# The small products of head pairs, chained in the order in which they are issued

## The chip, the cores and the metric

The kernel runs on one core of a Trainium2 chip. A time is the number of device microseconds (us) of one execution; of several executions the median is given. In the profile PE is TensorE, DVE is VectorE, ACT is ScalarE, POOL is GpSimd and SP is SyncE, whose queue issues most of the transfers.

## The reference: one hybrid decoder layer

The input x has 256 tokens of 2048 features, all float32. The layer is

```
x = x + 0.5 * swiglu(rms_norm(x))                       # feed-forward 1, inner width 5632
p = rms_norm(x) @ w_in                                  # all projections of the mixer
y_attn = sliding_window_attention(q, k, v, sinks)       # 16 heads of 64, 4 key heads, window 128
y_rwkv = rwkv7_time_mix(p_rwkv)                         # 16 heads of 64, a recurrence over tokens
x = x + (gate_a * (y_attn @ w_a) + gate_r * (y_rwkv @ w_r)) @ w_out
x = x + cross_attention(rms_norm(x), rms_norm(mem))     # 4 heads of 128 into 256 memory rows
x = x + 0.5 * swiglu(rms_norm(x))                       # feed-forward 2
out = rms_norm(x)
```

The recurrence of one head keeps a 64 x 64 state S and does, token by token,

```
sa = S a_t ;  S = S * w_t + sa b_t^T + v_t k_t^T ;  y_t = S r_t
```

with the decay w and the rate a taken from two low-rank products (`tanh(xw) @ w2` and `xa @ a2`, both of rank 64).

## The kernel before

**The stream.** Nearly all of the arithmetic is products of 256 tokens with large weight matrices. Weights are loaded in pieces of 2 or 4 x 128 rows by 512 columns, each split by ScalarE and VectorE into a rounded part and a remainder (lines 311 and 312), and each product of a piece is three matmuls of 128 rows and 512 columns (lines 399, 400 and 401, in `times`). These three lines are called the stream below. The two feed-forwards use a scheme with seven instead of eight block products; they are not touched.

**What runs beside it.** All smaller work of the mixer (attention, the recurrence, transposes, norms) is written as generators that `bg`, an `Interleave`, advances by one step after each half piece of the stream. So the order in the source is a mixture: a few small matmuls, then six of the stream, then small ones again. The build then has a scheduler that puts the instructions of each engine into a final order by its own estimate of when their operands and buffers are ready; it may move a small matmul past matmuls of the stream. `tc.issue_after(ins)` gives it one more rule: what is traced in the block comes after `ins` in the order of that engine. It adds no wait on a semaphore, and it does not ask that the two be neighbours.

**Head pairs.** Heads are 64 wide, and a feature tile has 128 partitions, so two heads lie in one tile: head e = 0 in partitions 0 to 63 and head e = 1 in 64 to 127. A product that contracts over one head's 64 features uses only 64 rows of the array: rows 0 to 63 (called the low half, L) for e = 0 and rows 64 to 127 (the high half, H) for e = 1. Each head of a pair has its own PSUM bank. At four places such products come in pairs:

- `attend`, line 856: attention scores, per key head and query block 2 x 2 products of 128 or 256 columns (32 in all);
- `decay_and_rate`, line 994: the low-rank products, 4 x 4 products of 256 columns (16);
- `removal_keys`, line 1087: the matrix of the token-by-token system that is later inverted, 4 x 8 products of 128 columns (32);
- `pair`, line 1226: three products for each head, head pair and half of the tokens, 16 groups of 6 products of 128 columns (96).

Operands here are plain float32, and each such product is carried out as two matmul instructions, each with its own weight load: the profile counts 192 matmuls for the 96 products of line 1226.

**What reads them.** After each group VectorE reads the two banks, e = 0 first: line 862 (scores, which the softmax follows), line 1093 (multiplication by the mask), line 1231 (multiplication by three masks, into `mk`); for the low-rank products it is ScalarE, line 1001. The first reader on TensorE of `mk` is line 1240. The banks of a group come from rings: `mm()` has three buffers, `tr()` has two, and both are shared with other small work, so the first product into a bank can have to wait for the last reader of the bank's former content.

**Other small matmuls** beside these groups: lines 596 and 895 are transposes; 903 is the attention output (64 columns of the array each); 1168, 1240 to 1289 are the rest of the recurrence; they use all 128 rows.

The loop of the recurrence, before:

```
for m, (x1, x2) in enumerate(((kh, ah), (kh, rh), (bh, rh))):
    for e, r in enumerate(rows):
        pe.matmul(b[e][:, m * P : (m + 1) * P], x1[r, j, cs_], x2[r, j, cs_], ...)
```

## Time and profile before

| | |
|---|---|
| median of 3 runs | 2266.49 us (2264.76 to 2267.68) |
| the profiled execution | 2266.59 us, of which the span of its instructions 2264.9 us |
| granted TensorE clock in it | 0.999 |
| PE busy | 2248.1 us, 99% of the span |
| DVE, ACT, POOL busy | 1742.6, 1212.8, 129.4 us |
| DMA | 434.63 MB, mean 192 GB/s |

The mixer's scores are computed at about 768 to 817 us from the span's start, the low-rank products at 835 to 849, line 1087 at 895 to 936, and line 1226 at 1090 to 1261.

How it is read: a row of the timeline gives the start, the duration, the engine, the line, the operation, the tiles, the rows and columns of the array, and how many instructions were merged into the row; in square brackets stands idle time of the engine before it, with what ended it. The ends of matmuls are modelled, and they overlap the next ones, so it is the distance from start to start that tells what a matmul costs. A row of the view by stretches gives the stretch (from : to), its length, the busy time of the engine and in brackets how many of its instructions touch the stretch, then the clock and the DMA share.

### The profile page before, as it was taken

The numbers are of one execution on the slowest core, as the hardware profiler recorded it, in microseconds if no ns is written. First come the engines' busy times: TensorE is split into PE (matmuls) and PEld (weight loads), VectorE is DVE, ScalarE is ACT, GpSimd is POOL, SyncE is SP. The second block draws the span as 40 slices with busy tenths as digits, with TensorE's granted clock in tenths as the row PEclk, the third lists the DMA queues.
The fourth block names the chain that finished last, engine by engine and source line by source line (L and its number), as shares of the span: only waits on it lengthen the run. The fifth ranks groups of instructions, "written<-read, shape, count | busy, mean of one in ns | idle before, by whom it ended". The sixth has DMA issues, their size and how long they took to land.

```text
span 2264.9 us, 28302 instructions
## 1 busy us (share of the span) xinstructions
PE 2248.1 (99%) x10588; PEld 1843.7 (81%) x10588; DVE 1742.6 (77%) x2120; ACT 1212.8 (54%) x1611; POOL 129.4 (6%) x184
## 2 busy tenths in 40 slices
PE   9999999999999999999999999999999999999998
PEld 7888888888888778888888888888888888888886
DVE  7988988888986567795444566647898888898887
ACT  6555555545555576444344446556555455555554
POOL 1000000000000002201220030001000000000002
PEclk9999999999999999999999999999999999999999
DMA  7666665566666545766433577647665665666664
GB/s 244 213 223 196 204 205 190 184 215 196 200 205 195 142 142 161 236 209 195 116 108 88 170 258 235 194 159 261 195 204 186 205 204 186 194 197 204 202 201 155
DMA packets 219435, 434.63 MB, mean 192 GB/s; under 512 B 13745, under 2 KB 15873, under 8 KB 219297
## 3 DMA queue, kind: packets, MB, share of 16 engines
q1 hardware_dynamic: 210768, 406.37, 56.2%
q0 software_dynamic: 7952, 25.65, 3.6%
q8 instruction: 83, 1.36, 0.2%
q10 hardware_dynamic: 576, 0.79, 0.1%
q14 instruction: 56, 0.45, 0.1%
HBM read 419.65 MB, written 13.11 MB: 191 GB/s over the span
## 4 chain that ended last, share of the span: by engine, by line
PE 92%; DVE 3%; DMA 2%; issue 1%; ACT 1%; SPq 0%; POOLq 0%; POOL 0%; ACTq 0%; DVEq 0%
PE acc L399 19%; PE acc L400 19%; PE acc L401 19%; PE mm L400 8%; PE mm L401 8%; PE mm L399 8%; PE tr L596 2%; PE tr L400 2%; PE tr L401 2%; PE tr L399 1%; DVE lo L312 1%; PE mm L1257 1%; PE tr L1226 1%; DMA raw<-in_ffn_w_up_dram 1%; ACT hi L311 1%
## 5 line engine op out<-in xcount | busy, mean ns | idle before, releaser
L311 ACT CAST hi<-raw 128x1024 fp32r<-128x1024 f32 (+1 forms) x770 | 763.6, 1000 | 787.8 <-PE acc L401 394.5
L312 DVE TENSOR_TENSOR lo<-raw,hi 128x1024 fp32r<-128x1024 f32 (+1 forms) x770 | 891.2, 1168 | 370.5 <-ACT hi L311 369.2
L399 PE MATMUL acc<-hi,xhi 128*128 128x512 f32 (+1 forms) x1196 | 477.0, 400 | 1.3 <-ACT hi L311 1.0
L400 PE MATMUL acc<-lo,xhi 128*128 128x512 f32 (+1 forms) x1196 | 465.6, 389 | 0.8 <-DVE lo L312 0.8
L401 PE MATMUL acc<-hi,xlo 128*128 128x512 f32 (+1 forms) x1196 | 464.9, 389 | 0.0
L399 PEld LDWEIGHTS acc<-hi,xhi 128*128 128x128 f32 x1196 | 225.0, 188 | 51.3 <-issue 5.4
L401 PEld LDWEIGHTS acc<-hi,xlo 128*128 128x128 f32 x1196 | 225.0, 188 | 47.0 <-issue 0.6
L400 PEld LDWEIGHTS acc<-lo,xhi 128*128 128x128 f32 x1196 | 225.3, 188 | 46.3 <-issue 2.7
L336 ACT CAST thi<-raw 128x1024 fp32r<-128x1024 f32 x160 | 166.0, 1051 | 72.2 <-DVE raw L331 35.6
L337 DVE TENSOR_TENSOR tlo<-raw,thi 128x1024 fp32r<-128x1024 f32 x160 | 192.8, 1219 | 1.1 <-ACT thi L336 1.1
L400 PE MATMUL acc<-lo,hhi 128*128 128x512 f32 x404 | 157.9, 391 | 0.0
L401 PE MATMUL acc<-hi,hlo 128*128 128x512 f32 x404 | 157.8, 391 | 0.0
L399 PE MATMUL acc<-hi,hhi 128*128 128x512 f32 x404 | 157.2, 392 | 0.0
L399 PE MATMUL mm<-hi,xhi 128*128 128x512 f32 x380 | 149.1, 392 | 0.0
L400 PE MATMUL mm<-lo,xhi 128*128 128x512 f32 x380 | 148.1, 390 | 0.0
L401 PE MATMUL mm<-hi,xlo 128*128 128x512 f32 x380 | 148.1, 390 | 0.0
L331 DVE TENSOR_TENSOR raw<-raw 128x1024 f32<-128x1024 f32 x80 | 97.6, 1220 | 23.6 <-DMA raw<-in_ffn_w_up_dram 22.1
L400 PEld LDWEIGHTS acc<-lo,hhi 128*128 128x128 f32 x404 | 75.8, 188 | 17.5 <-DVE lo L312 2.3
L399 PEld LDWEIGHTS acc<-hi,hhi 128*128 128x128 f32 x404 | 75.9, 188 | 16.0 <-DVE x L554 0.9
L401 PEld LDWEIGHTS acc<-hi,hlo 128*128 128x128 f32 x404 | 75.9, 188 | 15.3
L400 PEld LDWEIGHTS mm<-lo,xhi 128*128 128x128 f32 x380 | 71.4, 188 | 15.3 <-DVE lo L312 0.4
L401 PEld LDWEIGHTS mm<-hi,xlo 128*128 128x128 f32 x380 | 71.3, 188 | 14.7
(374 smaller groups left out, 3409.5 us busy)
## 6 DMA issues: line engine op xcount, KB each, us to landing
raw<-in_ffn_w_gate_dram SPq DMA_DIRECT2D x167, 512.0 KB, 3.8
raw<-in_ffn_w_up_dram SPq DMA_DIRECT2D x160, 512.0 KB, 4.7
raw<-in_ffn_w_down_dram SPq DMA_DIRECT2D x152, 512.0 KB, 4.8
raw<-in_w_in_dram SPq DMA_DIRECT2D x136, 512.0 KB, 3.7
raw<-in_w_out_dram SPq DMA_DIRECT2D x32, 512.0 KB, 4.5
raw<-in_ffn_w_down_dram SPq DMA_DIRECT2D x12, 1024.0 KB, 5.1
raw<-in_ffn_w_up_dram SPq DMA_DIRECT2D x8, 1024.0 KB, 6.3
raw<-in_w_proj_attn_dram SPq DMA_DIRECT2D x16, 512.0 KB, 3.8
```

The source lines that it names most:

```text
L311: newest["act"] = act.copy(hi[:, s], raw[:, s])
L312: newest["dve"] = dve.tensor_tensor(lo[:, s], raw[:, s], f32(hi[:, s]), ALU.subtract)
L331: dve.tensor_tensor(ta[:], raw[:, 1:3], raw[:, 0:2], ALU.subtract)
L336: act.copy(hi[:, s], t[:])
L337: dve.tensor_tensor(lo[:, s], t[:], f32(hi[:, s]), ALU.subtract)
L399: pe.matmul(o, xh, hi, start=first, stop=False, **how)
L400: pe.matmul(o, xh, lo, start=False, stop=False, **how)
L401: pe.matmul(o, xl, hi, start=False, stop=last, **how)
L596: pe.transpose(b[:, o : o + P], tok[:, t, col : col + P], ident[:])
L1226: pe.matmul(b[e][:, m * P : (m + 1) * P], x1[r, j, cs_], x2[r, j, cs_], start=True, stop=True,)
L1257: pe.matmul(vb[:, o : o + P][:, r], lhs(e), rhs[:, r], start=first and e == 0, stop=True, **ek,)
```

## The change

The products of each of the four places are handed to a new function, which gives each product after the first the rule to come after the one before it. And the head with e = 1 now comes first in each pair. The number of products, their operands, their results and the readers stay the same.

```diff
+    def by_turns(products):
+        prev = None
+        for args in products:
+            with tc.issue_after(prev.ins) if prev else nullcontext():
+                prev = pe.matmul(*args, start=True, stop=True)
 
@@ attend
-            for c in range(2):
-                for e in range(2):
-                    r = slice(64 * e, 64 * e + 64)
-                    pe.matmul(
-                        b[e][:, c * w : (c + 1) * w], qt[kv // 2][r, 2 * (kv % 2) + c, tq],
-                        kd[r, kv, :w], start=True, stop=True,
-                    )
+            by_turns(
+                (
+                    b[e][:, c * w : (c + 1) * w],
+                    qt[kv // 2][64 * e : 64 * e + 64, 2 * (kv % 2) + c, tq],
+                    kd[64 * e : 64 * e + 64, kv, :w],
+                )
+                for c in range(2) for e in (1, 0)
+            )
@@ decay_and_rate
-                    for i in range(2):
-                        for e in range(2):
-                            r, c = slice(64 * e, 64 * e + 64), (4 * h + q + i) * P
-                            pe.matmul(
-                                b[e][:, i * T : (i + 1) * T], wa[r, c : c + P], xwa[r, :],
-                                start=True, stop=True,
-                            )
+                    by_turns(
+                        (
+                            b[e][:, i * T : (i + 1) * T],
+                            wa[64 * e : 64 * e + 64, (4 * h + q + i) * P : (4 * h + q + i + 1) * P],
+                            xwa[64 * e : 64 * e + 64, :],
+                        )
+                        for i in range(2) for e in (1, 0)
+                    )
@@ removal_keys
-                for j in range(4):
-                    for e in range(2):
-                        r = slice(64 * e, 64 * e + 64)
-                        pe.matmul(
-                            b[e][:, j * P : (j + 1) * P], at_[h][r, j, cs_], bt[h][r, j, cs_],
-                            start=True, stop=True,
-                        )
+                by_turns(
+                    (
+                        b[e][:, j * P : (j + 1) * P], at_[h][64 * e : 64 * e + 64, j, cs_],
+                        bt[h][64 * e : 64 * e + 64, j, cs_],
+                    )
+                    for j in range(4) for e in (1, 0)
+                )
@@ pair
-                for m, (x1, x2) in enumerate(((kh, ah), (kh, rh), (bh, rh))):
-                    for e, r in enumerate(rows):
-                        pe.matmul(
-                            b[e][:, m * P : (m + 1) * P], x1[r, j, cs_], x2[r, j, cs_],
-                            start=True, stop=True,
-                        )
+                by_turns(
+                    (b[e][:, m * P : (m + 1) * P], x1[r, j, cs_], x2[r, j, cs_])
+                    for m, (x1, x2) in enumerate(((kh, ah), (kh, rh), (bh, rh)))
+                    for e, r in ((1, rows[1]), (0, rows[0]))
+                )
```

## The prediction

> **What bounds the kernel now.** I read the page first (busy time, then the chain that ended last), then the stretch of the recurrence, then TensorE's timeline around one group of each kind.

> ```profile
> PE 2248.1 (99%) x10588; PEld 1843.7 (81%) x10588; DVE 1742.6 (77%) x2120; ACT 1212.8 (54%) x1611; POOL 129.4 (6%) x184
> ...
> PE 92%; DVE 3%; DMA 2%; issue 1%; ACT 1%; SPq 0%; POOLq 0%; POOL 0%; ACTq 0%; DVEq 0%
> ```

> TensorE is busy all the time and carries 92% of the chain. In the view by stretches the recurrence, where 96 of the 176 touched products lie, is tighter still:

> ```profile
> 1085.00:1265.00 180.00, 179.83 (x1175) 149.52 (x1174) 80.53 (x106) 76.58 (x172) 22.90 (x38) 1.00 0.35 99
> ```

> Busy times stand here in the order PE, PEld, DVE, ACT, POOL: TensorE lacks 0.17 of 180 us, VectorE works 80.53. So there the time is the sum of distances from one matmul's start to the next, and a shorter distance moves all that follows.

> **What a group costs.** One group of line 1226 that already alternates, in TensorE's timeline:

> ```profile
> 1089.71 0.39 PE L401 MATMUL acc<-hi,xlo 128*128 128x512 f32 x1
> 1090.03 0.49 PE L1226 MATMUL tr<-at,aa 64*128 64x128 f32 x4
> 1090.36 0.39 PE L1226 MATMUL tr<-rt,aa 64*128 64x128 f32 x4
> 1090.58 0.39 PE L1226 MATMUL tr<-rt,kk 64*128 64x128 f32 x4
> 1090.90 0.50 PE L399 MATMUL acc<-hi,xhi 128*128 128x512 f32 x1
> 1091.23 0.39 PE L400 MATMUL acc<-lo,xhi 128*128 128x512 f32 x1
> 1091.47 0.40 PE L401 MATMUL acc<-hi,xlo 128*128 128x512 f32 x1
> ```

> The stream steps by about 0.23. Into the group it takes 0.32, out of it 0.33 to the second matmul: a visit to 64-row products costs its own stretch (first start to the next product's start) and about 0.20 beside (0.32 + 0.33 less two steps). Now the stretches, one row each, PE's count also taking in neighbours that run into the stretch. Recurrence:

> ```profile
> 1090.03:1090.90 0.87, 0.87 (x13) 1.00 0.87 306
> 1093.37:1094.24 0.87, 0.87 (x8) 1.00 0.89 346
> 1095.36:1096.22 0.86, 0.86 (x7) 1.00 0.00 0
> 1098.66:1100.22 1.56, 1.56 (x14) 1.00 0.24 93
> 1120.98:1122.60 1.62, 1.62 (x14) 1.00 0.05 10
> 1126.29:1127.90 1.61, 1.61 (x13) 1.00 0.00 0
> 1145.27:1146.69 1.42, 1.42 (x15) 1.00 0.00 0
> 1164.81:1165.22 0.41, 0.41 (x3) 1.00 0.33 80
> 1165.64:1166.28 0.64, 0.64 (x6) 1.00 0.73 147
> 1166.94:1167.80 0.86, 0.86 (x7) 1.00 1.04 331
> 1188.25:1189.82 1.57, 1.57 (x14) 1.00 0.57 220
> 1205.58:1206.77 1.19, 1.19 (x14) 1.00 0.49 33
> 1207.66:1208.53 0.87, 0.87 (x13) 1.00 1.00 386
> 1213.37:1214.93 1.56, 1.56 (x13) 1.00 0.00 0
> 1255.57:1255.98 0.41, 0.41 (x3) 1.00 0.00 0
> 1259.79:1260.65 0.86, 0.86 (x7) 1.00 0.72 210
> ```

> Six products in turns (first row) take 0.87; three of one half alone also take 0.86 to 0.87: the partner is free. Three of one half and then three of the other take 1.42 to 1.62, or 1.19 where H could start under the L products; one product alone takes 0.41, two 0.64. The scheduler of before turned the source's L H L H L H into L L L H H H in ten of the 16 groups (in three of these with other matmuls between the parts), since the second head's bank comes free later. What such a group costs hangs on when that is.

> **The change, part by part.** No instruction is added or removed on any engine; POOL's and SP's queues are in the same order, transfers included. As built, a few casts and small operations of ACT and DVE change places with a neighbour. What moves is on TensorE. [...]

> *Recurrence (line 1226).* As built, six of the 16 groups are H L H L H L without a gap; in ten the first H stands alone, one to 14 other matmuls follow, then L H L H L together. In the ten that costs 0.41 + 0.87 and two visits, 1.68 in all (the five last ones by three products of one half, the partner free). Group by group, visits included, before and after:

> - first, fourth, ninth, 14th, 15th: in turns before and after, 1.07, no change;
> - second (0.87 and 0.86 apart): 2.13 to 1.68, -0.45; third: 1.76 to 1.68, -0.08; fifth: 1.82 to 1.68, -0.14; sixth: 1.81 to 1.07, -0.74; seventh: 1.62 to 1.68, +0.06;
> - eighth and 16th (0.41, 0.64 and 0.86 apart, three visits): 2.51 to 1.68, -0.83 each;
> - tenth and 13th: 1.77 and 1.76 to 1.68, -0.17 together;
> - eleventh (1.19): 1.39 to 1.68, +0.29; twelfth (0.87): 1.07 to 1.68, +0.61. These two lose.

> Sum -2.3. The wait for the second bank doesn't go: in 1098.66 to 1100.22 it lay behind three L products; now other matmuls lie there, and L after them comes no earlier than the H of before did.

> *Matrix to invert (line 1087).* Two visits for each half of the heads, and VectorE's first masked multiply in each:

> ```profile
> 895.85:897.83 1.98, 1.98 (x25) 1.00 0.18 69
> 898.76:899.85 1.09, 1.09 (x9) 1.00 0.45 120
> 931.75:933.73 1.98, 1.98 (x25) 1.00 0.19 68
> 934.44:935.53 1.09, 1.09 (x9) 1.00 0.46 118
> ```

> ```profile
> 898.03 0.68 DVE L1093 TENSOR_TENSOR lt<-mm,mask_l 128x512 f32<-128x512 f32 x1
> ```

> Before: eight products in turns and four L (1.98), one stream matmul, then four H, which wait for that multiply (it ends at 898.71, they start at 898.76; the second time they start at 934.44, alike). After, as built: nine in turns, four or five stream matmuls, then seven in turns beginning with L. Nine in turns are five of one half: 0.86 + two more products of 0.22 (0.86 less 0.64) = 1.30. The second visit still waits for the same multiply and still takes 1.09 (four of one half), but three and four more stream matmuls are done by then: 7 x 0.23 = -1.6.

> *Scores (line 856) and low rank (line 994).* Stretches of the second and fourth scores, and of one low-rank group:

> ```profile
> 781.62:782.47 0.85, 0.85 (x9) 1.00 0.00 0
> 783.92:785.51 1.59, 1.59 (x9) 1.00 0.70 186
> 810.78:812.07 1.29, 1.29 (x12) 1.00 0.09 27
> 835.64:836.71 1.07, 1.07 (x10) 1.00 0.76 145
> ```

> All four low-rank groups alternate before and after: 0. So do the first and third scores. In the second, L H H of 256 columns (1.59) becomes L H L like the low-rank row (1.07), less 0.20 for a visit that now stands among stream matmuls: -0.3. In the fourth, two L of 256 columns at the end of a visit (1.29) become one (0.85): -0.4. Two blocks of line 903 are also split by a stream matmul before and whole after; by the 0.20 of a visit that is worth between 0 (the second half waits for its copy instead) and -0.4; I take -0.2, as nothing tells.

> Sum: -2.3 - 1.6 - 0.7 - 0.2 = -4.8 us. Its ends: with nothing for line 903 -4.6, with all of it -5.0; the two losing groups and the visits are sums of like rows and have no wider bounds of their own. The profiled execution took 2266.59 (its span 2264.9 and 1.7 around), 0.1 over the median of the three runs, so 2261.8 against it and 2261.7 against the median, 0.21% less.

> [...] The 64-row visits of the recurrence go from 21 to 26. [...] Counted alone it would make the time 5 x 0.20 = 1.0 us longer; it is in the sum already.

> **What could hide or undo it.** The two mask multiplies of line 1231 both come after the group now, where that of e = 0 could run beside H H H before:

> ```profile
> 1091.01 1.02 DVE L1231 TENSOR_TENSOR mk<-tr,mask 128x384 f32<-128x384 f32 x2
> ```

> ```profile
> 1184.95 1.23 DVE L312 TENSOR_TENSOR lo<-raw,hi 128x1024 fp32r<-128x1024 f32 x1 [3.00 <-ACT hi L311]
> ```

> ```profile
> 1186.70 0.32 PE L1240 MATMUL tr<-vtok,mk 128*128 128x64 f32 x1 [0.17 <-DVE mk L1231]
> ```

> In the first group both end at 1092.03, 1.13 after the group's stretch ended; as built the shortest way from a changed group to line 1240 is five stream matmuls (0.33 + 4 x 0.23 = 1.25). That is covered, by 0.12 at the least.

> **Rivals.**
> - *Slower: the masks are late.* Line 1240 waits wherever VectorE is in one of its long subtractions (line 312) when the group ends. One such case, of the ninth group, is the last two rows above. If it meets all eleven regrouped ones in full (1.13 of mask work behind a subtraction of 1.23, less the 1.25: 1.1 us each), that is +12.1 - 4.8 = +7.3: 2273.8. It decides from 0.44 us per group on. Against it: VectorE is idle for more than half of this stretch. 0.12.
> - *Partly lost: it does not do what it says.* The chain orders the products and does not make them neighbours; ten first products stand alone, and were the L after them to wait for its bank, or the last scores, which come eight stream matmuls later, to hold up the transposes at 825.83, half would go:

> ```profile
> 825.83 0.76 PE L895 MATMUL tr<-ident,s 128*128 128x128 f32 x5 [0.80 <-DVE s L889]
> ```

>   -2.4: 2264.1. For it: that wait exists, and the scores' softmax is a chain of VectorE and ScalarE. Against: the reduction of the other block comes ahead as built. 0.18.
> - *More:* the wait of 0.80 goes too, and the two blocks of line 903 give all of 0.4: -4.8 - 0.8 - 0.2 = -5.8: 2260.7. For it: the work on VectorE between the scores and the transposes moves ahead. 0.25.

> **Numbers.** The forecast, 2261.7 give or take 1.2, has 0.45. A measurement tells about 0.2%, 4.5 us, so "faster" begins at 2262.0: most of the forecast's part (0.28) and all of "more" (0.25) are faster, 0.53. The rest of it (0.17) and "partly lost" are the same, 0.35. Slower: 0.12. The range reaches over the forecast, "more" with 2 us for waits outside, and "partly lost" up to 2267: 2258.5 to 2267.

> **What the profile after would show.** Right: the sum of line 1226's stretches about 2 us shorter, no L L L H H H; at 1087 the second visit seven in turns and the same wait; feed-forwards unchanged. Wrong: idle time before line 1240 put down to `mk`, before the second part of a group put down to a copy or mask, or before line 895 longer than 0.80.

## The result, and the profile after

The changed kernel takes 2260.45 us (median of 10 runs, 2258.33 to 2262.48), the kernel before, run beside it, 2265.47 (10 runs, 2264.18 to 2267.68): 5.0 us less, a ratio of 0.9977 with a 95% interval of 0.9967 to 0.9987. The forecast was 4.8 us less. The profiled execution took 2258.33 us, its span 2256.6.

Lines below the new function are 8 to 10 further down than before: the stream is now lines 407 to 409, and all chained products stand under line 177, inside `by_turns`. The page's busy times and its chain, after:

```profile
PE 2240.6 (99%) x10588; PEld 1836.1 (81%) x10588; DVE 1740.8 (77%) x2120; ACT 1213.3 (54%) x1611; POOL 130.9 (6%) x184
...
PE 95%; DVE 3%; issue 1%; ACT 1%; DMA 1%; SPq 0%; POOLq 0%; POOL 0%; ACTq 0%; DVEq 0%
```

TensorE does the same 10588 matmuls, is busy 7.5 us less, and is still busy 99% of the time: the gain lies in how densely its products start, not in idle time taken away.

**Where it came from.** Both kernels issue the same number of matmul instructions in all of these stages, so the time from the start of one fixed instruction, counted from the start of the kernel and standing a few instructions away from a stage, to the start of the next such one can be compared directly. Worked out so from the records of the trace, profiled execution against profiled execution (us):

| stretch | before | after less before | predicted |
|---|---|---|---|
| first feed-forward and what precedes the scores | 765.81 | -1.05 | 0 |
| scores, line 903, low rank | 127.31 | -1.08 | -0.9 |
| matrix (line 1087 of before) | 49.42 | -1.58 | -1.6 |
| matrix to recurrence | 145.21 | 0.00 | 0 |
| recurrence (line 1226 of before) | 176.48 | -1.97 | -2.3 |
| **mixer, the four together** | 498.42 | **-4.63** | **-4.8** |
| all behind the recurrence | 990.84 | -2.57 | 0 |

The profiled pair is 8.3 us apart, more than the medians; the 3.6 us outside the mixer are taken up in the experiments.

**The groups.** Stretches of TensorE after (from : to, length, busy time of PE and the matmul instructions that touch it, clock, DMA share, GB/s), in this order: two visits of the scores, the second low-rank group, the two visits of the first half of the matrix, then the recurrence's first group, its second, sixth, eighth and twelfth:

```profile
783.54:784.60 1.06, 1.06 (x8) 1.00 0.54 185
808.78:809.63 0.85, 0.85 (x9) 1.00 0.09 27
837.23:838.56 1.33, 1.33 (x9) 1.00 0.81 211
893.72:895.03 1.31, 1.31 (x20) 1.00 0.22 83
896.63:897.71 1.08, 1.08 (x14) 1.00 0.47 146
1086.32:1087.19 0.87, 0.87 (x14) 1.00 0.99 351
1089.66:1090.08 0.42, 0.42 (x4) 1.00 1.00 390
1091.66:1092.52 0.86, 0.86 (x12) 1.00 0.00 0
1122.58:1123.72 1.14, 1.14 (x13) 1.00 0.86 212
1159.98:1160.40 0.42, 0.42 (x3) 1.00 0.25 78
1161.98:1162.84 0.86, 0.86 (x11) 1.00 1.06 407
1202.67:1203.09 0.42, 0.42 (x4) 1.00 0.02 5
1203.52:1204.38 0.86, 0.86 (x11) 1.00 0.00 0
```

The reader should see four things. The ten split groups are one product alone (0.42) and then five in turns (0.86 or 0.87), as forecast. The twelfth group, which was whole before (0.87), is now split and loses, also as forecast. The sixth, whole and in turns, takes 1.14 and not 0.87. And the second low-rank group, in turns as before, takes 1.33 where it took 1.07: its second product starts at 837.50, when ScalarE has read its bank (line 1011); in the run with the scores alone, further down, the same group takes 1.33 too, so this is a price of the scores having moved ahead. In the first half of the matrix the second visit still waits for the same VectorE multiplication; in the second half (931.63) no idle time is left before it:

```profile
896.63 1.16 PE L177 MATMUL mm<-kk,at 64*128 64x128 f32 x14 [0.41 <-DVE lt L1103]
```

TensorE's waits in the mixer, in the view of who waited for whom (total, times, longest), before and then after:

```profile
PE tr L895 <- DVE s L889: 0.8, 1, 0.8
PE mm L1087 <- DVE lt L1093: 0.6, 2, 0.4
PE tr L903 <- ACT pt L898: 0.6, 1, 0.6
PE acc L399 <- DVE ga L1140: 0.2, 1, 0.2
PE tr L1240 <- DVE mk L1231: 0.2, 1, 0.2
```

```profile
PE tr L904 <- DVE s L898: 0.7, 1, 0.7
PE tr L912 <- ACT pt L907: 0.6, 1, 0.6
PE mm L177 <- DVE lt L1103: 0.4, 1, 0.4
PE acc L407 <- DVE ga L1150: 0.2, 1, 0.2
PE tr L1249 <- DVE mk L1240: 0.2, 1, 0.2
```

They are the same five, together 0.3 us shorter. The masks `mk` are not late: 0.2 before, 0.2 after.

### The profile page after: what moved, and what is told of

It reads as the page before. It is cut to its first block, busy times and chain, and to the rows that moved or that the text cites. A ratio compares the mean times of both kernels' runs of the same rounds, so it can differ in the third digit from the quotient of the medians.

```text
span 2256.6 us, 28302 instructions
## 1 busy us (share of the span) xinstructions
PE 2240.6 (99%) x10588; PEld 1836.1 (81%) x10588; DVE 1740.8 (77%) x2120; ACT 1213.3 (54%) x1611; POOL 130.9 (6%) x184
## 4 chain that ended last, share of the span: by engine, by line
PE 95%; DVE 3%; issue 1%; ACT 1%; DMA 1%; SPq 0%; POOLq 0%; POOL 0%; ACTq 0%; DVEq 0%
PE acc L407 19%; PE acc L409 19%; PE acc L408 19%; PE mm L408 8%; PE mm L409 8%; PE mm L407 8%; PE tr L604 2%; PE tr L408 2%; PE tr L409 2%; PE tr L407 2%; PE mm L1266 1%; DVE lo L320 1%; PE tr L177 1%; PE mm L177 1%; ACT hi L319 0%
```

## The experiments

Three questions were open. Do the four places add up, or does part of the gain come from elsewhere in the program? Is it the turns themselves that pay, or what the chain does to the time at which the second head's bank is needed? And what is a group worth whose bank is free? A ratio stands with its interval; a kernel without a ratio is one profiled execution.

### One place at a time

**Recurrence alone**: `by_turns` at line 1226 of before; the three other places written as before.

> The chain at line 1226 (recurrence) alone; the other three places as before. Theory of the distances: the change is worth, place by place, what the starts of TensorE's matmuls say, and nothing else. Then the recurrence, 4858th to 5600th matmul, is 2.0 us shorter than before, as in the changed kernel, and the scores and the matrix to invert are as before to 0.1; time 2.0 below before. Rival, the outside: the 3.7 us by which the profiled execution of the changed kernel was also shorter outside the mixer come from the change; then the feed-forwards get shorter here too, by something like 3.7 x 2.0/4.6 = 1.6, in all -3.6.

**Matrix alone** (line 1087 of before).

> The chain at line 1087 (matrix to invert) alone. Distances: the two places together 1.6 us shorter, all else in the mixer as before to 0.1; time 1.6 below before. Outside: feed-forwards shorter as well, by 1.3, in all -2.9.

**Scores alone** (line 856).

> The chain at line 856 (scores) alone. Distances: the attention stretch up to the low-rank products 1.1 us shorter (of it -1.0 in the second block, +0.4 in the fourth, -0.5 behind it, where the last transposes wait), all else as before; time 1.1 below before. Outside: feed-forwards shorter by 0.9 as well.

**Low rank alone** (line 994), where only the leading head changes: a control.

> The chain at line 994 (low rank) alone: as built the same visits with H first. Distances: nothing in any stretch of the mixer, 0 +- 0.1; the time differs from before by what feed-forwards differ between executions. If the order of the two heads counted (H first cheaper than L first), the four visits of 1.07 would change.

The edit is the same for each. For the recurrence alone, against the changed kernel, at one of the three places that go back:

```diff
@@ attend
-            by_turns(
-                (
-                    b[e][:, c * w : (c + 1) * w],
-                    qt[kv // 2][64 * e : 64 * e + 64, 2 * (kv % 2) + c, tq],
-                    kd[64 * e : 64 * e + 64, kv, :w],
-                )
-                for c in range(2) for e in (1, 0)
-            )
+            for c in range(2):
+                for e in range(2):
+                    r = slice(64 * e, 64 * e + 64)
+                    pe.matmul(
+                        b[e][:, c * w : (c + 1) * w], qt[kv // 2][r, 2 * (kv % 2) + c, tq],
+                        kd[r, kv, :w], start=True, stop=True,
+                    )
```

Measured, less before's profiled execution, by the same stretches (us):

| | after | recurrence | matrix | scores | low rank |
|---|---|---|---|---|---|
| scores, line 903, low rank | -1.08 | -0.04 | -0.07 | -1.02 | +0.05 |
| matrix | -1.58 | +0.01 | -1.57 | +0.02 | +0.01 |
| recurrence | -1.97 | -1.97 | -0.01 | -0.03 | -0.01 |
| mixer | -4.63 | -1.99 | -1.64 | -1.02 | +0.07 |
| first feed-forward | -1.05 | +1.45 | +0.97 | +0.53 | +1.68 |
| behind the recurrence | -2.57 | +4.73 | +0.47 | -0.74 | +0.05 |
| time, us (before beside them 2266.29) | | 2270.78 | 2266.38 | 2265.39 | 2268.39 |

Each part gives its own stretch what the whole change gives it, to a few hundredths, and nothing to the others; the four mixers add up to -4.58 against -4.63. So the gain is local. The total times of single executions don't follow, because the stretches outside differ by up to 5 us: the low-rank control, in which only the leading head changed, is 1.68 longer in the first feed-forward, because the granted clock was 0.67 and 0.76 in the two stretches of 3 us from 21 us on (3 x 0.33 + 3 x 0.24 = 1.7 us), where it was 1.00 in before's and after's execution. The 3.6 us by which the profiled pair differs outside the mixer lie within what executions differ by there, and no run ties them to the change; the medians, 5.0 us apart, hold little of them.

**The recurrence alone, once more**, since its time was 4.5 us over before's where 2 us less were due.

> The chain at line 1226 alone, as in x1_recur, once more and timed. In x1_recur the recurrence was 1.97 us shorter, but the stretch behind the mixer 4.73 us longer, with a wait of 1.90 us of TensorE for the normed x (line 1408 there) at 1379.5 and a granted clock of 0.71 and 0.73 in the 6 us behind it. If the parts add and that wait belongs to the one execution: recurrence again 1.97 us shorter, the stretch behind the mixer within 1.5 us of before, the median about 2 us under before's. If the regrouped products lead to that wait through VectorE's order: the wait of 1.9 us and the lower clock come again, and the median is the same as before's or some 2 us above.

The median is 2265.84 against 2267.21, ratio 0.9993 (0.9984 to 1.0002): 1.4 us less, though the interval includes no change. The recurrence is again exactly 1.97 shorter; the stretch behind the mixer is 1.15 longer, not 4.73. In TensorE's timeline the wait for the residual sum `x` behind the mixer, in the first execution and then in the second:

```profile
1379.53 0.33 PE L604 MATMUL tr<-ident,x 128*128 128x128 f32 x1 [1.90 <-DVE x L1408]
```

```profile
1378.60 0.33 PE L604 MATMUL tr<-ident,x 128*128 128x128 f32 x1 [1.60 <-DVE x L1408]
```

And the stretches around it, first execution, then second (the fifth column is the granted clock):

```profile
1377.00:1380.00 3.00, 0.96 (x4) 1.00 0.57 180
1380.00:1383.00 3.00, 2.87 (x12) 0.71 0.54 178
1383.00:1386.00 3.00, 3.00 (x12) 0.73 0.86 283
```

```profile
1380.00:1383.00 3.00, 3.00 (x16) 1.00 0.54 170
1383.00:1386.00 3.00, 3.00 (x15) 1.00 1.00 344
```

Both expectations were half right. The wait came in both executions of this kernel (2.2 and 1.9 us in all, against 0.6 in before's profiled execution and none in after's), so there one place alone paid back some of its gain at the next hand-over; the lower clock, worth 3 x 0.29 + 3 x 0.27 = 1.7 us, came in one execution alone. What makes `x` late there and not in the changed kernel was not followed further.

### The order of the heads

All four places in turns, but the low half first:

```diff
-                    for e, r in ((1, rows[1]), (0, rows[0]))
+                    for e, r in ((0, rows[0]), (1, rows[1]))
```

> All four places chained, but the low half first (the pairs in the order L H instead of H L). As built it has the same visits as the changed kernel with L and H exchanged. Distances: every stretch of the mixer as in the changed kernel to 0.1 us, the mixer 4.6 shorter than before. Rival, the head order: if H first is what pays (for instance since VectorE reads the low half first), the scores, the matrix or the recurrence lose part of their -1.1, -1.6 and -2.0.

One execution took 2259.36 us; mixer -4.58, recurrence -1.97, matrix -1.55, scores -1.07. Which head leads made no difference here.

### The chain without the turns

The same chains at all four places, but each head's products one after the other, L L L H H H:

```diff
                     (b[e][:, m * P : (m + 1) * P], x1[r, j, cs_], x2[r, j, cs_])
+                    for e, r in enumerate(rows)
                     for m, (x1, x2) in enumerate(((kh, ah), (kh, rh), (bh, rh)))
-                    for e, r in ((1, rows[1]), (0, rows[0]))
```

> The same chain, but with all products of the low half first and then all of the high half (L L L H H H in place of turns), at all four places. Distances: in the recurrence 13 groups at about 1.56 + 0.20 and three split ones (2.13, 2.51, 2.51) are 30.0 us instead of 25.5, +4.5 against before; low rank +0.6 to +0.8 for each of four visits, +2.8; scores about +2; matrix about 0, since it then makes fewer visits. The mixer +9 against before, the time about 2274.5. Rival, the chain as such (that the scheduler no longer mixes, whatever the order in the chain): the time would be at or below that of before.

Measured: 2266.12 us, ratio 1.0003 (0.9995 to 1.0012), no change, where 2274.5 was expected. The recurrence is 1.49 us longer than before (4.5 expected), the stretch with the scores 0.85 longer, the matrix 0.74 shorter; the low-rank groups, now queued by halves, are not longer at all (1.07 each). Three groups of the recurrence:

```profile
1090.88:1092.07 1.19, 1.19 (x13) 1.00 0.90 324
1099.84:1101.40 1.56, 1.56 (x14) 1.00 0.13 49
1121.68:1123.30 1.62, 1.62 (x14) 1.00 0.00 0
```

Two kinds of L L L H H H are to be seen: 1.19 in the first group, which had taken 0.87, and the 1.56 and 1.62 of groups that were in this order before. The expectation had taken the second price for all. What parts the two kinds is the subject of the next sections.

### A free bank for the second head

In before and after both banks of a group come from `tr()`, a ring of two, so the second head has to wait until the ring's other buffer is read. The changed kernel's sixth group shows it: its first product starts at 1122.58, its second, of the other head, only at 1122.86, 0.05 after this read by ScalarE of a buffer of that ring has ended:

```profile
1122.43 0.38 ACT L1260 COPY nt<-tr 128x256 f32<-128x256 f32 x1
```

Here the pair takes one bank from each ring, without any chain:

```diff
-                b = [tr() for _ in range(2)]
+                b = [mm(), tr()]
```

> The kernel before without any chain; only at line 1226 the two banks of a group come from two rings (the first from the ring of three, the second from the ring of two) instead of both from the ring of two. As built 12 of the 16 groups are then L H L H L H, two are L and H L H L H, two are still by halves. Theory that the second bank, freed late, is what splits the heads: the recurrence is 12 x 1.07 + 2 x 1.68 + 2.51 + 1.6 = 20.3 us instead of 25.5, -5.2, more than the chain gave there (-2.0), and scores, low rank and matrix are as before; time 2260.3. Rival: that the ring of three is short too, so that the stages of line 1257 wait for banks instead: the recurrence gains less than 2 and shows idle time of TensorE before line 1257.

2258.92 us (2257.51 to 2261.84), ratio 0.9969 (0.9958 to 0.9981); recurrence -6.12, three times what the chain gives it. Most groups are now whole and in turns without being told to. The sixth and the eleventh group:

```profile
1123.20:1124.07 0.87, 0.87 (x14) 1.00 0.00 0
1200.12:1201.51 1.39, 1.39 (x13) 1.00 0.17 62
```

**Both**, the chain and these banks:

> The changed kernel with the two banks of line 1226 from two rings. As built 14 of 16 groups are H L H L H L together and two are H and L H L H L: 18 visits instead of 26. Distances: the recurrence is 14 x 1.07 + 2 x 1.68 = 18.3 us instead of 25.5, -7.2 against before, -4.9 against the changed kernel; scores and matrix as in the changed kernel (-1.1, -1.6). Time 2265.5 - 9.9 = 2255.6. Rival: waits for the ring of three take it back, as above.

2255.5 us (2254.11 to 2256.15), ratio 0.9951 (0.9938 to 0.9965); recurrence -7.60. All but two of the 16 groups are whole, and the eleventh, which the banks alone left at 1.39, is too. Here the sixth, the eleventh and the twelfth:

```profile
1123.03:1123.90 0.87, 0.87 (x14) 1.00 0.00 0
1199.64:1200.51 0.87, 0.87 (x13) 1.00 0.00 0
1201.41:1202.28 0.87, 0.87 (x14) 1.00 0.97 367
```

The sixth group's 1.14 of the changed kernel is 0.87 here: it had been waiting for its bank. Eighteen visits are left of 26.

**The matrix too**: in addition its second group of each two takes the second bank from the other ring.

```diff
-                b = [mm() for _ in range(2)]
+                b = [mm(), mm() if c == 0 else tr()]
```

> The changed kernel with free second banks at two places: at line 1226 the banks of a group from two rings (as in the run with chain and banks), and at line 1087 the high half's bank of the second half of the tokens from the ring of two. As built the matrix to invert is then one visit of 16 products in turns for each half of the heads instead of two. Theory of the late bank (what splits the pairs is that the second bank comes free late; where both are free the pairs run together): the matrix takes 0.86 + 5 x 0.22 + 0.20 = 2.16 each instead of 1.98 + 1.09 + 0.40 and waits of 0.60 and 0.39, -3.6 against before; the recurrence -7.6 and the scores -1.0 as measured. Mixer -12.2, time 2265.8 - 12.2 = 2253.6. Rival: VectorE's masked multiplies, now behind all 16 products, hold the stream (idle time put down to line 1093 or to a bank of the ring of two): matrix no better than -1.6, time 2255.5.

2254.64 us (2254.03 to 2257.81), ratio 0.9946 (0.9932 to 0.9959): the lowest median, 13.3 us under before's 2267.89 beside it. The two intervals overlap; that it is faster than the kernel above is read from the stretches alone. The matrix is -3.34 and has become one visit of 16 products each time, without the wait for VectorE; the first of the two:

```profile
896.54:898.53 1.99, 1.99 (x33) 1.00 0.24 91
```

The mixer is -11.43, against -10.18 for chain and banks; in it, +0.63 is a loss between matrix and recurrence.

**The same banks without any chain**:

> The kernel before without any chain, with the same free banks at lines 1226 and 1087. As built the matrix is 16 products in turns in one visit (low half first) and the recurrence is as in the run with banks alone. Late bank: matrix -3.6, recurrence -6.1, scores 0: mixer -9.7, time 2256.1; the chain is then worth only the rest, 1.0 in the scores and 1.5 in the recurrence. Rival, the chain is needed for the turns: matrix and recurrence well short of that.

2258.93 us, ratio 0.9965 (0.9952 to 0.9977); matrix -3.34, recurrence -6.11, the same as with its banks alone. But between the two, +3.58, so that the profiled mixer is only 5.91 shorter. The time is lost at one place. TensorE there, and the stretches behind it:

```profile
989.66 0.50 PE L399 MATMUL acc<-hi,xhi 128*128 128x512 f32 x1 [1.76 <-DVE ga L1140]
```

```profile
988.00:991.00 3.00, 1.34 (x6) 1.00 0.73 197
991.00:994.00 3.00, 3.00 (x9) 0.51 1.00 313
994.00:997.00 3.00, 3.00 (x13) 0.92 1.00 320
```

The gate product `ga` (line 1140) stands on VectorE behind the token-by-token substitution of lines 1115 and 1120, and the substitution started when its data had come back through DRAM, at 958.43, later than before's 957.13 although the matrix was done sooner (why they came later was not followed):

```profile
958.43 0.16 DVE L1115 TENSOR_TENSOR tmp<-xt,dl 128x1 f32<-128x1 f32 x1 [2.61 <-DMA dl<-ld]
```

```profile
957.13 0.15 DVE L1115 TENSOR_TENSOR tmp<-xt,dl 128x1 f32<-128x1 f32 x1
```

So the wait for `ga` grew from 0.2 to 1.76 (1.5 us), and the clock then fell to 0.51 for some 3 us (3 x 0.49 + 3 x 0.08 = 1.7 us): 3.2 of the 3.58. With the chain the same wait is 0.8 us, and the granted clock behind it stayed at 1.00: this is the 0.63. The median of the kernel without the chain, 9.0 us under before, suggests that most of its executions lose less than the profiled one. By the medians, taken side by side, the chain is worth 4.3 us on top of these banks (2258.93 to 2254.64); 1.1 of it lie in the scores and 1.5 in the recurrence.

### The turns themselves, with the bank free

Banks as in the kernel with the lowest median, chains by halves as in L L L H H H:

> All four places chained by halves (all low products, then all high ones), with the same free banks at lines 1226 and 1087. It leaves the order L L L H H H and takes away the wait for the bank. Look-ahead theory (TensorE starts a product of the other half up to four matmul instructions ahead of its place): L L L H H H takes 1.19 and not 1.56 in all 13 whole groups, the recurrence is 13 x 1.39 + 2 x 1.68 + 1.91 = 23.3 instead of 25.5, -2.2 against before; the low-rank visits stay at 1.07. Strict order (the first H not before the last L has started): 1.42 or more in each group, the recurrence +0.8 against before. In both the matrix is between -1 and -3 and the scores at about +0.9, as in the run by halves.

One execution, 2263.66 us; recurrence -3.11, against -7.61 for the same banks in turns. Of the 13 whole groups 12 now take 1.19 or 1.20 and one 1.40, where groups in turns take 0.87. The price of the order alone is thus 0.32 a group, and in groups of 1.56 to 1.62 the late bank was the larger part. The recurrence gained 0.9 us more than the look-ahead estimate of the expectation (-2.2); that is not accounted for. How a group in halves can take 1.20, where two times three products of one half would take 2 x 0.87, is in TensorE's timeline of its first group. L writes the bank from `mm`, H the one from `tr`; queued are six instructions of L (two each of at, rt and kk) and then six of H:

```profile
1090.34 0.48 PE L177 MATMUL mm<-at,aa 64*128 64x128 f32 x2
1090.67 0.27 PE L177 MATMUL mm<-rt,aa 64*128 64x128 f32 x1
1090.67 0.37 PE L177 MATMUL tr<-at,aa 64*128 64x128 f32 x1
1090.78 0.27 PE L177 MATMUL mm<-rt,aa 64*128 64x128 f32 x1
1090.89 0.27 PE L177 MATMUL tr<-at,aa 64*128 64x128 f32 x1
1090.89 0.27 PE L177 MATMUL mm<-rt,kk 64*128 64x128 f32 x1
1091.00 0.27 PE L177 MATMUL tr<-rt,aa 64*128 64x128 f32 x1
1091.00 0.27 PE L177 MATMUL mm<-rt,kk 64*128 64x128 f32 x1
1091.11 0.27 PE L177 MATMUL tr<-rt,aa 64*128 64x128 f32 x1
1091.22 0.38 PE L177 MATMUL tr<-rt,kk 64*128 64x128 f32 x2
```

## Why the prediction was right, and where it was off

- *What bounds the kernel*: right. TensorE lacked nothing before and lacks nothing now; a shorter distance between starts moved everything behind it, and each part's gain stands in the total.
- *Recurrence, -2.3*: measured -1.97. By parts of the stretch, second and third group -0.55 (forecast -0.53), seventh +0.04 (+0.06), eighth -0.83 (-0.83), ninth and tenth -0.09 (-0.09), eleventh to 13th +0.79 (+0.82), 16th -0.74 (-0.83). The mis-sized term is the sixth group, -0.74: fourth to sixth together gave -0.59 instead of -0.88, since the sixth is whole but takes 1.14 with its bank late. The prediction took 0.87 for every group in turns in one visit, also for one whose bank might come late; with a free bank the group does take 0.87.
- *The two losing groups*: right. The chain, by holding the other products behind a first H, splits groups that had been dense.
- *Matrix, -1.6*: measured -1.58, by the mechanism named: the second visit starts when the same multiplication allows it, and seven more stream matmuls are done by then.
- *Scores and line 903, -0.9, and low rank, 0*: together -1.08. The 1.06 and the 0.85 of the two visits came as forecast. That the sum came so near is partly luck: up to the low rank the stretch is 1.39 shorter, and the low-rank groups are 0.32 longer, which the prediction put at nothing. By its order of issue the low rank does cost nothing (alone +0.05); it is again a bank that comes late.
- *Masks late*, the slower rival: didn't happen; 0.2 us of waiting for `mk` before and after.
- *Partly lost* and *more*: neither as a whole. The wait ahead of the transposes went from 0.8 to 0.7 us.
- The five more visits, which alone would have cost 1.0 us, were in the sum. With visits of 0.20 the sum of the recurrence's stretches gives -2.0 for the changed kernel (26 visits, 18.29 us of stretches, against 21 and 21.29), and -7.2 for chain and banks (18 visits, 14.71), where -1.97 and -7.60 were measured.
- *Order of the starts*: in the kernel by halves with free banks a matmul of the other half started at 1090.67, ahead of three that were queued before it and started at 1090.78 to 1091.00 (last section). No term of the sum was worked out from an order of starts within a group.

What the prediction did not see is that the order of issue is the smaller lever. It named the cause, a bank that comes late, and then treated it as given; the banks alone gave 6.1 us in the recurrence against the chain's 2.0.

## What to carry to other kernels

Where paired products of the two row halves do not run side by side, look first at when the second head's PSUM bank comes free: in this kernel the groups fed from two rings mostly ran densely by themselves (recurrence -6.12 us), while the chain on late banks mostly moved the gap (-1.97 us). With the banks free, the chain then made the last few groups dense (-7.60 us; the eleventh went from 1.39 to 0.87). And read the gain of a local change in its own stretch, since the single executions here differed by up to 5 us elsewhere.

## What the runs showed of the hardware

- **A matmul of the other row half started ahead of three queued before it.** The rows above (1090.67 for the seventh instruction, 1090.78 to 1091.00 for the fourth to sixth) show starts out of the queue's order: in this group the first H instruction overtook three L instructions. This is why a group by halves took 1.19 with a free bank, where 1.42 or more had been expected of a strict order. In the low rank by halves, where four L instructions and then four H are queued, a group takes 1.07 (840.33 to 841.40) as in turns.
- **Two waits of 1.90 and 1.76 us were followed by a lower clock, two of 1.7 and 1.60 us were not.** Behind the waits of 1.90 and 1.76 us above, the granted clock was 0.71 and 0.73 in two stretches of 3 us (1380 to 1386), and 0.51 and 0.92 in two others (991 to 997), which cost a further 1.7 us each time. The length of a wait alone did not decide it. Behind the one of 1.60 us, and behind one of 1.7 us between 1905 and 1911 in the first execution of the recurrence alone, the stretches show 1.00. And two waits of 1.2 and 0.8 us near 20 us from the start were followed by 0.67 and 0.76 in the low-rank control, and by 1.00 in that execution, which had the same two. The longest single wait ahead of these three falls was 1.90 us. What decides was not tested.
